# Gate and up products of two FFNs: plain block products against Strassen's form for two of four k-group pairs

## The chip, the core and the metric

The kernel runs on one core of one Trainium2 chip. The metric is the device time of one execution in microseconds; the kernel before takes 2469.53 us (median of three runs, 2468.38 to 2471.1). TensorE multiplies, VectorE (DVE) and ScalarE (ACT) work on elements, GpSimd (POOL) does little here, and the queue of SyncE (SP) issues all weight loads.

## The reference

Two transformer blocks run one after the other on x of 256 tokens by 2048 features, in fp32. The first has three mixers, then a gated FFN with a short convolution, then a gated per-layer input; the second has two mixers and a SwiGLU FFN, and a final norm. The change concerns the FFNs:

```python
def conv_ffn(x, w_gate, w_up, conv_w, conv_b, w_down):
    hg = x @ w_gate                      # [256, 2048] @ [2048, 5632]
    hg = conv_general_dilated(hg, conv_w, ..., feature_group_count=hg.shape[-1]) + conv_b
    return (gelu(hg) * (x @ w_up)) @ w_down

c = rmsnorm(h, ffn_norm); h = h + conv_ffn(c, w_gate, w_up, conv_w, conv_b, w_down)
...
h = rmsnorm_2(x, ffn_norm_w)
x = x + (silu(h @ w_gate) * (h @ w_up)) @ w_down
```

## The kernel before

Every product with a weight matrix is made in fp32 accuracy out of fp32r matmuls. An operand is split in two parts: hi is the value rounded to fp32r, lo is the rest. The product is hi x hi + hi x lo + lo x hi, three matmuls (lines 156 to 158), all added up in one PSUM bank.

The tokens are two tiles of 128 (m = 0, 1). The activations lie feature-major as 16 k-tiles xT of [128, 256], each already split. A weight is read in chunks of 512 columns and k groups of two k-tiles: a weight block is [128, 2 x 512] of fp32, 512 KB. `product` (line 160) walks the 8 k groups of a chunk. For each block SP loads it into one of seven buffers (three "raw", four "t4k"), ACT writes the rounded copy `whi` (line 133), VectorE writes `wlo = raw - whi` (line 134), and TensorE does 12 matmuls of 128x512: two k-tiles, two token tiles, three parts. There are three buffers each of `whi` and `wlo`.

An FFN has 11 chunks u of 512 hidden features. A unit makes gate chunk u and up chunk u, 8 blocks each (`conv_unit` line 556, `swiglu_unit` line 575); `evacuate` (line 236) takes a result out of PSUM scaled with the token's norm factor r. `hidden` then transposes it, applies convolution and GELU (or the SwiGLU product) and splits it into stationary tiles `hid`. Units go in groups (0,1), (2,3), ..., (10). After the two units of a group the down product of the group before is made: four output chunks of 8 blocks, each added to h by VectorE (line 541). Transposes and other small work are generators that `pump` advances at each weight block, so they fall between the blocks.

The order on each engine is set when the program is built: a scheduler places the instructions by priority (a split has high priority) and by its own estimate of when operands are ready. On the chip each engine runs its own list in that order, with semaphores for the waits. PSUM has eight banks: four "acc" for products, four "tp" for transposes and small products.

Of the kernel before, what the change touches and what calls it, by code (L numbers as in the profile page):

```python
# [17 lines left out]
P = 128  # L18
T = 256
# [34 lines left out]
def two_blocks_kernel(ctx: ExitStack, tc: tile.TileContext, A: dict, out: bass.AP):  # L54
# [105 lines left out]
    def product(w, c, xs, k0=0, order=None, width=2):  # L160
        """acc[m] = xs^T @ w[k-tiles k0.., chunk c] for both token tiles m."""
        n = w.widths[c]
        acc = [psum("acc"), psum("acc")]
        groups = order if order is not None else list(range(len(xs) // KG))
        for gi, g in enumerate(groups):
            while any(x is None for x in xs[g * KG : g * KG + KG]):
                pump()
            hi, lo = split_weight(w, c, k0 // KG + g)
            for j in range(KG):
                xhi, xlo = xs[g * KG + j]  # L170
                first = gi == 0 and j == 0
                last = gi == len(groups) - 1 and j == KG - 1
                wh, wl = hi[:, j * n : (j + 1) * n], lo[:, j * n : (j + 1) * n]
                for m in range(2):
                    three_products(acc[m][:, :n], xhi, xlo, m, wh, wl, first, last)
            pump(width)
        return acc

    def stationary(src, tag, scale=None):
        """Exact two-part split of a feature-major [128, 256] operand."""  # L180
        hi = new([P, T], tag, 32, F32R)
        lo = new([P, T], tag, 32, F32R)
        if scale is None:
            act(hi, src, AF.Copy)  # L184
            dve.tensor_tensor(lo, src, hi.bitcast(F32), op=ALU.subtract)
        else:
            act(hi, src, AF.Copy, scale=scale)
            dve.scalar_tensor_tensor(lo, src, scale, hi.bitcast(F32), ALU.mult, ALU.subtract)
        return hi, lo

    def transpose_pair(views, dst=None):
        """Two token-major [128, 128] views side by side, feature-major, in PSUM."""
        t = psum() if dst is None else dst
        for m, v in enumerate(views):
            pe.transpose(t[:, m * P : (m + 1) * P], v, ident)  # L195
        return t[:, :T]

    def norm_chunk(c, g, st):
        """Sums of squares of h[c], and its k-tiles, transposed and scaled by the gain."""
        for kk in range(4):  # L200
            if kk == 2:
                yield 1
            k = c * 4 + kk
            t = transpose_pair([h[c][:, m, kk * P : (kk + 1) * P] for m in range(2)])
            st.xs[k] = stationary(t, "xT", g[:, k : k + 1])
# [6 lines left out]
    class NormState:  # L212
        def __init__(self):
# [12 lines left out]
    def token_r(st):  # L226
# [99 lines left out]
    def hgrn_head(hh):  # L326
# [182 lines left out]

    # --- MOBA: one block of 256 keys, so the own block is the whole causal range  # L510
    def moba_bias(hh):
# [30 lines left out]

    def residual_norm(w, xin, g, order=None):
        """h += xin @ w, and the transposed scaled h for the next products."""
        st = NormState()
        for c in range(NCH):
# [3 lines left out]

    ahead[0] = True
    xs, r = residual_norm(W["out"], mix, G_FFN)

    # ================================================================== block 1: conv FFN
    def conv_unit(u, xs, r):
        gt = evacuate(product(W["gate"], u, xs), r)
        ut = evacuate(product(W["up"], u, xs), r)

# [15 lines left out]

    def swiglu_unit(u, xs, r):
        sg = evacuate(product(W["gate2"], u, xs), r, func=AF.Silu)
        acc = product(W["up2"], u, xs)
        for m in range(2):
            dve.scalar_tensor_tensor(sg[:, m], acc[m], r[:, m : m + 1], sg[:, m], ALU.mult, ALU.mult)

# [10 lines left out]

    def ffn(unit, down, xs, r, g):
        groups = [(0, 1), (2, 3), (4, 5), (6, 7), (8, 9), (10,)]
        prev = None
        st = NormState() if g is not None else None

        def drain(u0, hid, last):
            if last and g is None:
                return final_rows(down, u0, hid)
            for c in range(NCH):  # L600
# [11 lines left out]
        drain(*prev, True)  # L612
        return (st.xs, st.r) if g is not None else None
# [47 lines left out]
    w = W["in2"]  # L661
    # --- GLA
    gm = load_matrix("gla_m", 1152, "cm")
# [385 lines left out]
```

## Time and profile before

| | |
|---|---|
| median of three runs | 2469.53 us |
| span of the profiled execution | 2464.9 us |
| TensorE matmul busy | 2441.0 us, 11424 instructions |
| VectorE busy | 1421.2 us, 1767 instructions |
| ScalarE busy | 1219.1 us, 1705 instructions |
| granted TensorE clock, mean | 0.999 |
| read from memory | 444.76 MB, mean 181 GB/s |

The profile records one execution. Its own device time isn't listed beside it; its span runs from the first to the last instruction and is 4.6 us shorter than the median. Times are in microseconds from the start of the span, means of single instructions in ns. A matmul's recorded duration (about 0.39 us) is longer than the distance to the next one, since matmuls are pipelined; the distance is what counts for throughput.

### The profile page before, as it was taken

What the parts mean: (1) busy time and instruction counts of PE and PEld (TensorE: products, weight loads), DVE (VectorE), ACT (ScalarE), POOL (GpSimd) and SP (SyncE); (2) the same over time, 40 slices, a digit from 0 to 9 for tenths busy, and PEclk for the clock granted to TensorE, in tenths of its full rate; (3) what the DMA queues carried; (4) which work ended last, traced back from release to release, by engine and by line L of the source; (5) the groups of instructions that cost most, each with busy time, mean ns of one, the idle gap of its engine ahead of it and who ended that gap; (6) DMA issues with size and microseconds to landing.
All of it is one profiled execution on the core that took longest, in us unless ns stands there. A gap on an engine that the chain in (4) does not pass through costs nothing.

```text
span 2464.9 us, 30001 instructions
## 1 busy us (share of the span) xinstructions
PE 2441.0 (99%) x11424; PEld 2015.9 (82%) x11424; DVE 1421.2 (58%) x1767; ACT 1219.1 (49%) x1705; POOL 20.6 (1%) x26
## 2 busy tenths in 40 slices
PE   9999999999999999999999999999999999999998
PEld 7878888888888888888887888788888888888886
DVE  6786565555555465555656755655545545454556
ACT  6545454455445454544556555654444443434444
POOL 0000000000000000000000000000000000000000
PEclk9999999999999999999999999999999999999999
DMA  7544565555555656555545465555565555655554
GB/s 241 145 144 151 179 205 187 186 184 185 186 191 182 195 179 193 187 186 186 183 152 179 153 197 186 165 160 186 191 191 188 189 190 191 191 188 189 188 195 141
DMA packets 130654, 448.86 MB, mean 182 GB/s; under 512 B 14860, under 2 KB 19852, under 8 KB 130510
## 3 DMA queue, kind: packets, MB, share of 16 engines
q1 hardware_dynamic: 130510, 446.95, 57.1%
q8 instruction: 89, 1.46, 0.2%
q14 instruction: 55, 0.45, 0.1%
HBM read 444.76 MB, written 2.13 MB: 181 GB/s over the span
## 4 chain that ended last, share of the span: by engine, by line
PE 94%; DVE 2%; DMA 1%; issue 1%; ACT 1%; SPq 0%; POOL 0%; POOLq 0%; DVEq 0%; ACTq 0%
PE acc L158 30%; PE acc L156 30%; PE acc L157 29%; PE tp L195 2%; DVE wlo L134 1%; ACT whi L133 1%; DMA mbias<-vdr 1%; PE tp L358 0%; DMA raw<-in_w_down 0%; PE tp L860 0%; DVE t2k L835 0%; PE tp L845 0%; DMA raw<-in_w_in 0%; DMA h<-in_x 0%; DVE at L367 0%
## 5 line engine op out<-in xcount | busy, mean ns | idle before, releaser
L156 PE MATMUL acc<-whi,xT 128*128 128x512 f32 (+3 forms) x2400 | 935.8, 390 | 0.0
L158 PE MATMUL acc<-whi,xT 128*128 128x512 f32 (+3 forms) x2400 | 924.4, 385 | 0.0
L157 PE MATMUL acc<-wlo,xT 128*128 128x512 f32 (+3 forms) x2400 | 924.2, 385 | 0.0
L134 DVE TENSOR_TENSOR wlo<-raw,whi 128x1024 fp32r<-128x1024 f32 (+3 forms) x483 | 575.1, 1191 | 521.0 <-ACT whi L133 520.2
L133 ACT ACTIVATE whi<-raw 128x1024 fp32r<-128x1024 f32 (+3 forms) x483 | 498.8, 1033 | 590.0 <-PE acc L158 523.0
L134 DVE TENSOR_TENSOR wlo<-t4k,whi 128x1024 fp32r<-128x1024 f32 x353 | 432.7, 1226 | 439.6 <-ACT whi L133 439.3
L133 ACT ACTIVATE whi<-t4k 128x1024 fp32r<-128x1024 f32 x353 | 374.3, 1060 | 481.0 <-PE acc L158 461.1
L158 PEld LDWEIGHTS acc<-whi,xT 128*128 128x128 f32 x2400 | 451.1, 188 | 90.6 <-issue 0.9
L156 PEld LDWEIGHTS acc<-whi,xT 128*128 128x128 f32 x2400 | 451.3, 188 | 87.7 <-issue 2.9
L157 PEld LDWEIGHTS acc<-wlo,xT 128*128 128x128 f32 x2400 | 451.8, 188 | 86.3 <-DVE wlo L134 0.7
L156 PE MATMUL acc<-whi,hid 128*128 128x512 f32 x944 | 376.4, 399 | 0.0
L157 PE MATMUL acc<-wlo,hid 128*128 128x512 f32 x952 | 370.9, 390 | 0.0
L158 PE MATMUL acc<-whi,hid 128*128 128x512 f32 x944 | 370.3, 392 | 0.0
L158 PEld LDWEIGHTS acc<-whi,hid 128*128 128x128 f32 x944 | 177.2, 188 | 40.9
L157 PEld LDWEIGHTS acc<-wlo,hid 128*128 128x128 f32 x952 | 179.0, 188 | 37.6 <-DVE wlo L134 0.3
L156 PEld LDWEIGHTS acc<-whi,hid 128*128 128x128 f32 x944 | 177.5, 188 | 34.8 <-issue 0.4
L236 ACT ACTIVATE pj<-acc,r 128x512 f32<-128x512 f32 (+3 forms) x96 | 63.5, 662 | 41.2 <-PE acc L158 41.2
L541 DVE TENSOR_TENSOR h<-h,acc 128x512 f32<-128x512 f32 x104 | 67.2, 681 | 0.0
L195 PE MATMUL tp<-ident,pj 128*128 128x128 f32 x344 | 54.7, 273 | 1.2 <-DVE t2k L835 1.2
L195 PEld LDWEIGHTS tp<-ident,pj 128*128 128x128 f32 x344 | 43.4, 140 | 14.7 <-DVE t2k L835 1.6
L413 ACT ACTIVATE t2k<-t2k,col 128x256 f32<-128x256 f32 (+1 forms) x56 | 26.8, 480 | 23.7 <-DVE col L412 23.6
L184 ACT ACTIVATE hid<-t1k 128x256 fp32r<-128x256 f32 x44 | 18.3, 416 | 35.6 <-DVE t1k L570 35.6
(229 smaller groups left out, 1083.0 us busy)
## 6 DMA issues: line engine op xcount, KB each, us to landing
raw<-in_w_in SPq DMA_DIRECT2D x184, 512.0 KB, 3.6
t4k<-in_w_gate SPq DMA_DIRECT2D x100, 512.0 KB, 3.5
t4k<-in_w_up SPq DMA_DIRECT2D x100, 512.0 KB, 3.4
t4k<-in_w_down SPq DMA_DIRECT2D x96, 512.0 KB, 3.5
raw<-in_w_down SPq DMA_DIRECT2D x80, 512.0 KB, 3.4
raw<-in_w_gate SPq DMA_DIRECT2D x76, 512.0 KB, 3.5
raw<-in_w_up SPq DMA_DIRECT2D x76, 512.0 KB, 3.5
t4k<-in_w_out SPq DMA_DIRECT2D x37, 512.0 KB, 3.5
```

The source lines that it names most:

```text
L133: act(hi[:, :n], raw[:, :n], AF.Copy)
L134: dve.tensor_tensor(lo[:, :n], raw[:, :n], hi[:, :n].bitcast(F32), op=ALU.subtract)
L156: pe.matmul(o, xhi[:, tok], wh, start=first, stop=False)
L157: pe.matmul(o, xhi[:, tok], wl, start=False, stop=False)
L158: pe.matmul(o, xlo[:, tok], wh, start=False, stop=last)
L184: act(hi, src, AF.Copy)
L195: pe.transpose(t[:, m * P : (m + 1) * P], v, ident)
L236: act(t[:, m, :n], acc[m][:, :n], func, scale=r[:, m : m + 1])
L413: act(lg[:, a:b], lg[:, a:b], AF.Exp, bias=nm[:, m : m + 1], accum_out=sm[:, m : m + 1])
L541: dve.tensor_tensor(h[c][:, m], h[c][:, m], acc[m], op=ALU.add)
```

## The change

For units 2 to 10 of both FFNs gate and up of a chunk are made together in `pair_product`. The k groups are taken in pairs (gp, gp + 4), gp = 0..3. Pairs 0 and 2 stay plain ("straight"): four blocks of 12 matmuls into the banks p2, q4 (gate) and q3, x22 (up). Pairs 1 and 3 are "mixed". There the 2x2 block matrix of activations (rows: token tiles; columns: the two k groups) is multiplied with the 2x2 block matrix of weights b11, b12, b21, b22 (rows: the two k groups; columns: gate, up) by Strassen's seven products. VectorE forms sums of whole weight blocks in place: t1 = b11 + b12, t3 = b12 + b22, t2 = t1 + b22, t4 = t2 + b21. Seven blocks f11, f21, f22, ft1, ft3, ft2, ft4 are split and each is multiplied with one [128, 128] stationary pair per k-tile, 6 matmuls, into banks p1, p2, q3, q5, q7, q6, q4. All eight PSUM banks are in use during a unit. At its end nine operations of ACT and VectorE combine the banks into ca (gate) and cb (up), which ACT then scales by r in place.

The stationary combinations of activations are made once for each FFN by `strassen_operands` (four k-tile pairs, kept in four of the eight "pj" tiles) beside units 0 and 1, which stay plain. The down product of the group before is made in halves: two output chunks after each unit of a group, instead of four after the second. `norm_chunk` gets copies of h scaled by the norm factor of the norm before (rho) for the FFN norms, and the new r is divided by rho.

```diff
+    def split_raw(raw):
+        hi, lo = new([P, KG * 512], "whi", 3, F32R), new([P, KG * 512], "wlo", 3, F32R)
+        act(hi, raw, AF.Copy)
+        dve.tensor_tensor(lo, raw, hi.bitcast(F32), op=ALU.subtract)
+        return hi, lo
+    def pair_product(wa, wb, u, xs, sx):
+        p1, p2, q3, q5 = (psum("acc") for _ in range(4))
+        q6, q7, x22, q4 = (psum() for _ in range(4))
...
+        def products(bank, st, wt, stop):
+            (shi, slo), (hi, lo) = st, wt
+            for j in range(KG):
+                wh, wl = hi[:, j * 512 : (j + 1) * 512], lo[:, j * 512 : (j + 1) * 512]
+                pe.matmul(bank, shi(j), wh, start=id(bank) not in begun, stop=False)
+                begun.add(id(bank))
+                pe.matmul(bank, shi(j), wl, start=False, stop=False)
+                pe.matmul(bank, slo(j), wh, start=False, stop=stop and j == KG - 1)
...
+            last = gp == MIXED[-1]
+            b11, b12, b21, b22 = (load_weight(w_, u, g) for g in (gp, gp + half) for w_ in (wa, wb))
+            with tc.high_priority():
+                f11 = split_raw(b11)
+                t1 = b11
+                dve.tensor_tensor(t1, b11, b12, op=ALU.add)
+                f21 = split_raw(b21)
+                f22 = split_raw(b22)
+                t3 = b12
+                dve.tensor_tensor(t3, b12, b22, op=ALU.add)
+            products(p1, plain(gp, 0), f11, last)
+            products(p2, plain(gp + half, 0), f21, last)
+            products(q3, mixed(gp, 3), f22, last)
+            with tc.high_priority():
+                ft1 = split_raw(t1)
+                t2 = b22
+                dve.tensor_tensor(t2, t1, b22, op=ALU.add)
+                ft3 = split_raw(t3)
+                t4 = b21
+                dve.tensor_tensor(t4, t2, b21, op=ALU.add)
+            products(q5, mixed(gp, 0), ft1, last)
+            products(q7, mixed(gp, 2), ft3, last)
+            with tc.high_priority():
+                ft2 = split_raw(t2)
+            products(q6, mixed(gp, 1), ft2, last)
+            with tc.high_priority():
+                ft4 = split_raw(t4)
+            products(q4, plain(gp + half, 1), ft4, last)
+        ca, cb = chunk_tile(), chunk_tile()
+        with tc.high_priority():
+            a1, w_ = t2k(), t2k()
+            act(a1, p1, AF.Copy)
+            dve.tensor_tensor(ca[:, 0], a1, p2, op=add)
+            dve.tensor_tensor(a1, a1, q6, op=add)
+            dve.scalar_tensor_tensor(w_, a1, -1.0, q5, ALU.mult, add)
+            dve.tensor_tensor(cb[:, 0], w_, q3, op=add)
+            dve.tensor_tensor(a1, a1, q7, op=add)
+            dve.tensor_tensor(w_, w_, q7, op=sub)
+            dve.tensor_tensor(cb[:, 1], w_, x22, op=add)
+            dve.tensor_tensor(ca[:, 1], a1, q4, op=add)
...
         for us in groups:
             hid = [None] * (4 * len(us))
             for i, u in enumerate(us):
-                add_side(fill(hid, 4 * i, unit(u, xs, r)))
-            if prev is not None:
-                drain(*prev, False)
+                add_side(fill(hid, 4 * i, unit(u, xs, r, sx if u > 1 else None)))
+                if prev is not None:
+                    step = NCH // len(us)
+                    drain(*prev, range(i * step, (i + 1) * step))
```

How the order moves. On VectorE, where a unit's gate product follows a down product in the first FFN, the kernel before has one row a weight block (L134) and the two additions to h at the end of a down chunk (L541), nothing else:

```order
L134 TENSOR_TENSOR wlo_6833<-t4k_6830,whi_6832 128x1024
L134 TENSOR_TENSOR wlo_6851<-raw_6848,whi_6850 128x1024
L541 TENSOR_TENSOR h_5_70<-h_5_70,acc_6752 128x512
L541 TENSOR_TENSOR h_5_70<-h_5_70,acc_6753 128x512
L134 TENSOR_TENSOR wlo_6869<-raw_6866,whi_6868 128x1024
L134 TENSOR_TENSOR wlo_6887<-raw_6884,whi_6886 128x1024
L134 TENSOR_TENSOR wlo_6905<-t4k_6902,whi_6904 128x1024
```

In the kernel after, the first mixed pair of a unit reads as follows (L601 is the subtraction of a split; L645, L649, L656, L659 are t1, t3, t2, t4; the last row belongs to the next straight block):

```order
L601 TENSOR_TENSOR wlo_6034<-t4k_6025,whi_6033 128x1024
L645 TENSOR_TENSOR t4k_6025<-t4k_6025,t4k_6027 128x1024
L649 TENSOR_TENSOR t4k_6027<-t4k_6027,raw_6031 128x1024
L601 TENSOR_TENSOR wlo_6039<-t4k_6029,whi_6038 128x1024
L601 TENSOR_TENSOR wlo_6043<-raw_6031,whi_6042 128x1024
L656 TENSOR_TENSOR raw_6031<-t4k_6025,raw_6031 128x1024
L601 TENSOR_TENSOR wlo_6066<-t4k_6025,whi_6065 128x1024
L601 TENSOR_TENSOR wlo_6071<-t4k_6027,whi_6070 128x1024
L601 TENSOR_TENSOR wlo_6088<-raw_6031,whi_6087 128x1024
L659 TENSOR_TENSOR t4k_6029<-raw_6031,t4k_6029 128x1024
L601 TENSOR_TENSOR wlo_6098<-t4k_6029,whi_6097 128x1024
L134 TENSOR_TENSOR wlo_6110<-raw_6107,whi_6109 128x1024
```

Four of the eleven rows are sums; t1 and t3 stand before f21's subtraction, t2 before ft1's, t4 before ft4's. The second mixed pair of a unit, from t2 on, also holds combinations (L674 is ca, L675 a1 with q6, L676 w):

```order
L656 TENSOR_TENSOR raw_6185<-t4k_6179,raw_6185 128x1024
L674 TENSOR_TENSOR pj_6261<-t2k_6263,acc_5946 128x512
L601 TENSOR_TENSOR wlo_6220<-t4k_6179,whi_6219 128x1024
L601 TENSOR_TENSOR wlo_6225<-t4k_6181,whi_6224 128x1024
L601 TENSOR_TENSOR wlo_6242<-raw_6185,whi_6241 128x1024
L659 TENSOR_TENSOR raw_6183<-raw_6185,raw_6183 128x1024
L675 TENSOR_TENSOR t2k_6263<-t2k_6263,tp_5949 128x512
L676 SCALAR_TENSOR_TENSOR t2k_6264<-t2k_6263,acc_5948 128x512
L601 TENSOR_TENSOR wlo_6252<-raw_6183,whi_6251 128x1024
L134 TENSOR_TENSOR wlo_6283<-raw_6280,whi_6282 128x1024
```

The combination ca moved in ahead of ft1's subtraction, and a1 and w ahead of ft4's. On TensorE, before, a gate product begins right behind another product (acc_6978), its first block's matmuls in a row (acc_7126 and acc_7127 are the two token tiles):

```order
L157 MATMUL acc_6978<-wlo_7108,xT_4097 128x512
L158 MATMUL acc_6978<-whi_7107,xT_4098 128x512
L156 MATMUL acc_7126<-whi_7130,xT_3516 128x512
L157 MATMUL acc_7126<-wlo_7131,xT_3516 128x512
L158 MATMUL acc_7126<-whi_7130,xT_3517 128x512
L156 MATMUL acc_7127<-whi_7130,xT_3516 128x512
L157 MATMUL acc_7127<-wlo_7131,xT_3516 128x512
L158 MATMUL acc_7127<-whi_7130,xT_3517 128x512
```

After, at the end of a unit's second mixed pair (tp_5949 is q6's bank, tp_5952 q4's; tp_6316 takes over q6's bank; acc_6278 and acc_6279 are the down product's), the rows are:

```order
L619 MATMUL tp_5949<-whi_6241,pj_4228 128x512
L195 MATMUL tp_6316<-ident_63,pj_6261 128x128
L616 MATMUL tp_5952<-whi_6251,xT_4106 128x512
L156 MATMUL acc_6278<-whi_6282,hid_5192 128x512
L156 MATMUL acc_6279<-whi_6282,hid_5192 128x512
L618 MATMUL tp_5952<-wlo_6252,xT_4106 128x512
L619 MATMUL tp_5952<-whi_6251,xT_4107 128x512
L616 MATMUL tp_5952<-whi_6251,xT_4113 128x512
L618 MATMUL tp_5952<-wlo_6252,xT_4113 128x512
L619 MATMUL tp_5952<-whi_6251,xT_4114 128x512
L157 MATMUL acc_6278<-wlo_6283,hid_5192 128x512
```

A transpose of ca that writes into q6's former bank stands ahead of q4, and the first matmuls of the down product stand between q4's first and its other five, which need ft4's `wlo`.

## Rows read from the trace of the kernel before

**Rows 1.** The page's head: span, and busy time, share and instructions of each engine.
```profile
span 2464.9 us, 30001 instructions
PE 2441.0 (99%) x11424; PEld 2015.9 (82%) x11424; DVE 1421.2 (58%) x1767; ACT 1219.1 (49%) x1705; POOL 20.6 (1%) x26
```
**Rows 2.** Waits, whole span: engine, line, releaser: us in total, times, longest.
```profile
ACT whi L133 <- PE acc L158: 984.1, 612, 3.6
DVE wlo L134 <- ACT whi L133: 959.5, 733, 3.4
```
**Rows 3.** Timeline of TensorE, first FFN: start us, us, instruction (two stretches).
```profile
1001.26 0.40 PE L157 MATMUL acc<-wlo,xT 128*128 128x512 f32 x1
...
1003.57 0.40 PE L158 MATMUL acc<-whi,xT 128*128 128x512 f32 x1
...
1013.41 0.39 PE L158 MATMUL acc<-whi,xT 128*128 128x512 f32 x1
...
1020.89 0.39 PE L158 MATMUL acc<-whi,xT 128*128 128x512 f32 x1
```
**Rows 4.** Groups of VectorE and ACT by form: count, busy us, mean ns, idle before.
```profile
L134 DVE TENSOR_TENSOR wlo<-t4k,whi 128x1024 fp32r<-128x1024 f32 x353 | 432.7, 1226 | 439.6 <-ACT whi L133 439.3
L541 DVE TENSOR_TENSOR h<-h,acc 128x512 f32<-128x512 f32 x104 | 67.2, 681 | 0.0
L579 DVE SCALAR_TENSOR_TENSOR pj<-acc,r,pj 128x512 f32<-128x512 f32 x22 | 15.4, 743 | 0.0
L637 DVE TENSOR_TENSOR h<-h,pj 128x512 f32<-128x512 f32 x8 | 5.5, 687 | 0.0
L236 ACT ACTIVATE pj<-acc,r 128x512 f32<-128x512 f32 x88 | 59.8, 680 | 39.7 <-PE acc L158 39.7
```
**Rows 5.** Timeline of VectorE and ACT, w_out's and the first FFN's products.
```profile
382.89 1.28 DVE L541 TENSOR_TENSOR h<-h,acc 128x512 f32<-128x512 f32 x2
...
999.80 0.48 DVE L567 SCALAR_TENSOR_TENSOR t1k<-tp,cols,t1k 128x255 f32<-128x255 f32 x1
1000.32 0.48 DVE L568 SCALAR_TENSOR_TENSOR t1k<-tp,cols,t1k 128x254 f32<-128x254 f32 x1
...
1000.79 1.06 ACT L133 ACTIVATE whi<-t4k 128x1024 fp32r<-128x1024 f32 x1 [1.71 <-PE acc L158]
1001.75 0.40 ACT L569 ACTIVATE t1k<-t1k 128x256 f32<-128x256 f32 x1
...
1011.53 1.23 DVE L134 TENSOR_TENSOR wlo<-raw,whi 128x1024 fp32r<-128x1024 f32 x1 [0.35 <-ACT whi L133]
1012.67 0.41 DVE L570 TENSOR_TENSOR t1k<-t1k,tp 128x256 f32<-128x256 f32 x1
...
1021.32 1.06 ACT L133 ACTIVATE whi<-t4k 128x1024 fp32r<-128x1024 f32 x1 [1.61 <-PE acc L158]
...
1022.41 1.23 DVE L134 TENSOR_TENSOR wlo<-t4k,whi 128x1024 fp32r<-128x1024 f32 x1 [1.45 <-ACT whi L133]
```
**Rows 6.** Timeline at the kernel's start: VectorE, weight load, matmul.
```profile
7.30 1.22 DVE L134 TENSOR_TENSOR wlo<-raw,whi 128x1024 fp32r<-128x1024 f32 x1 [0.81 <-ACT whi L133]
...
8.58 0.29 PEld L157 LDWEIGHTS acc<-wlo,xT 128*128 128x128 f32 x1 [0.15 <-DVE wlo L134]
...
8.95 0.63 PE L157 MATMUL acc<-wlo,xT 128*128 128x512 f32 x1
```
**Rows 7.** Windows: engines' busy time, then granted clock, DMA share, GB/s.
```profile
115.00:130.00 15.00, 13.77 (x102) 12.85 (x101) 13.51 (x22) 9.28 (x19) 0.71 (x1) 1.00 0.56 169
999.90:1013.40 13.50, 13.50 (x66) 11.13 (x65) 10.73 (x19) 8.36 (x15) 0.00 (x0) 1.00 0.49 161
1560.00:1570.00 10.00, 8.67 (x50) 6.73 (x49) 8.60 (x25) 8.36 (x23) 0.00 (x0) 1.00 0.58 182
2455.00:2460.00 5.00, 1.40 (x7) 0.80 (x5) 2.60 (x7) 2.03 (x5) 0.56 (x1) 0.84 0.00 0
```
**Rows 8.** DMA issues: instructions, KB of each, median us to landing.
```profile
t4k<-in_w_gate SPq DMA_DIRECT2D x100, 512.0 KB, 3.5
```

More of the change, by code (lines that the diff above doesn't have):

```diff
@@ L198, in norm_chunk @@
     def norm_chunk(c, g, st):
+        rows = [h[c][:, m] for m in range(2)]
+        if st.rho is not None:
+            rows = [t2k(), t2k()]
+            for m in range(2):
+                act(rows[m], h[c][:, m], AF.Copy, scale=st.rho[:, m : m + 1])
         for kk in range(4):
@@ L203, in norm_chunk @@
             k = c * 4 + kk
-            t = transpose_pair([h[c][:, m, kk * P : (kk + 1) * P] for m in range(2)])
+            t = transpose_pair([rows[m][:, kk * P : (kk + 1) * P] for m in range(2)])
             st.xs[k] = stationary(t, "xT", g[:, k : k + 1])
@@ L231, in token_r @@
         pool.tensor_tensor(st.r, ms, mhalf[:, :2], op=ALU.pow)
+        if st.rho is not None:
+            inv = new([P, 2], "rinv", 2)
+            dve.reciprocal(inv, st.rho)
+            dve.tensor_tensor(st.r, st.r, inv, op=ALU.mult)
     def evacuate(acc, r, n=512, func=AF.Copy, dst=None):
@@ L541, in add_to_h, with residual_norm @@
             dve.tensor_tensor(h[c][:, m], h[c][:, m], acc[m], op=ALU.add)
[L543 to L545 removed]
+    def residual_norm(w, xin, g, rho, order=None):
+        st = NormState(rho)
         for c in range(NCH):
@@ L551, in two_blocks_kernel, with strassen_operands, make @@
     ahead[0] = True
[L552 to L557, printed above, removed]
+    xs, r = residual_norm(W["out"], mix, G_FFN, r)
+    def strassen_operands(xs):
+        sx = {}
+        def make():
+            for gp in MIXED:
+                for k in range(gp * KG, gp * KG + KG):
+                    while xs[k] is None or xs[k + 8] is None:
+                        yield 1
+                    yield 1
+                    a, b = t1k(), t1k()
+                    for t, (hi, lo) in ((a, xs[k]), (b, xs[k + 8])):
+                        dve.tensor_tensor(t, hi.bitcast(F32), lo.bitcast(F32), op=ALU.add)
+                    a11, a21, a12, a22 = a[:, :P], a[:, P:], b[:, :P], b[:, P:]
+                    fm = t2k()
+                    d, s2, s3, s4 = (fm[:, i * P : (i + 1) * P] for i in range(4))
+                    dve.tensor_tensor(d, a21, a22, op=ALU.subtract)
+                    dve.tensor_tensor(s2, d, a11, op=ALU.subtract)
+                    dve.tensor_tensor(s3, a11, a21, op=ALU.subtract)
+                    dve.tensor_tensor(s4, s2, a12, op=ALU.add)
+                    x = chunk_tile(F32R)
+                    act(x[:, 0], fm, AF.Copy)
+                    dve.tensor_tensor(x[:, 1], fm, x[:, 0].bitcast(F32), op=ALU.subtract)
+                    sx[k] = x
+        add_side(make(), 1)
+        return sx
@@ new lines, in two_blocks_kernel, with plain, mixed @@
+    MIXED = (1, 3)
+    def split_raw(raw):
[6 more added lines that the diff above has]
+        q6, q7, x22, q4 = (psum() for _ in range(4))
+        begun = set()
+        def products(bank, st, wt, stop):
[6 more added lines that the diff above has]
+                pe.matmul(bank, slo(j), wh, start=False, stop=stop and j == KG - 1)
+        def plain(g, m):
+            tok = slice(m * P, (m + 1) * P)
+            return lambda j: xs[g * KG + j][0][:, tok], lambda j: xs[g * KG + j][1][:, tok]
+        def mixed(gp, i):
+            fs = slice(i * P, (i + 1) * P)
+            return lambda j: sx[gp * KG + j][:, 0, fs], lambda j: sx[gp * KG + j][:, 1, fs]
+        half = KT // KG // 2
+        straight = [gp for gp in range(half) if gp not in MIXED]
+        for gp in range(half):
+            if gp in straight:
+                for w_, banks in ((wa, (p2, q4)), (wb, (q3, x22))):
+                    for g in (gp, gp + half):
+                        wt = split_weight(w_, u, g)
+                        for m in range(2):
+                            stop = banks[m] is x22 and g == straight[-1] + half
+                            products(banks[m], plain(g, m), wt, stop)
+                continue
+            last = gp == MIXED[-1]
[27 more added lines that the diff above has]
+        ca, cb = chunk_tile(), chunk_tile()
+        add, sub = ALU.add, ALU.subtract
+        with tc.high_priority():
[9 more added lines that the diff above has]
+            dve.tensor_tensor(ca[:, 1], a1, q4, op=add)
+        return ca, cb
@@ L559, in hidden, with conv_unit @@
+    def conv_unit(u, xs, r, sx):
+        if sx is None:
+            gt = evacuate(product(W["gate"], u, xs), r)
+            ut = evacuate(product(W["up"], u, xs), r)
+        else:
+            gt, ut = pair_product(W["gate"], W["up"], u, xs, sx)
+            for t in (gt, ut):
+                for m in range(2):
+                    act(t[:, m], t[:, m], AF.Copy, scale=r[:, m : m + 1])
         def hidden(kk):
@@ L573, in conv_unit, with swiglu_unit @@
         return hidden
-    def swiglu_unit(u, xs, r):
-        sg = evacuate(product(W["gate2"], u, xs), r, func=AF.Silu)
-        acc = product(W["up2"], u, xs)
+    def swiglu_unit(u, xs, r, sx):
+        if sx is None:
+            sg = evacuate(product(W["gate2"], u, xs), r, func=AF.Silu)
+            up = product(W["up2"], u, xs)
+        else:
+            sg, ut = pair_product(W["gate2"], W["up2"], u, xs, sx)
+            for m in range(2):
+                act(sg[:, m], sg[:, m], AF.Silu, scale=r[:, m : m + 1])
+            up = [ut[:, m] for m in range(2)]
         for m in range(2):
-            dve.scalar_tensor_tensor(sg[:, m], acc[m], r[:, m : m + 1], sg[:, m], ALU.mult, ALU.mult)
+            dve.scalar_tensor_tensor(sg[:, m], up[m], r[:, m : m + 1], sg[:, m], ALU.mult, ALU.mult)
         def hidden(kk):
@@ L595, in ffn, with drain @@
         st = NormState() if g is not None else None
[L597 to L600, printed above, removed]
+        sx = strassen_operands(xs)
+        def drain(u0, hid, chunks, last=False):
+            for c in chunks:
                 add_to_h(c, product(down, c, hid, k0=u0 * 4))
```

11 lines of the change are left out of this document (7 added, 4 removed).

## Prediction

> **What bounds the kernel now.** I read the page's head first, then the waits, then the timeline of TensorE in a unit of the first FFN. TensorE is busy for 2441.0 of 2464.9 us and VectorE for 1421.2 [rows 1]: the kernel is a stream of matmuls, and whatever shortens that stream counts in full as long as nothing else comes late. In the stretch with little beside the products 33 steps from one matmul to the next take 7.48 us, 0.227 each; where VectorE has other work too, ten take 2.31 us, 0.231 [rows 3]. I use p = 0.229 us for a 128x512 matmul. A weight block of 12 matmuls is then 2.75 us and four blocks 10.99 us.
>
> Next, what feeds TensorE. ACT rounds each weight block (whi), VectorE subtracts (wlo). ACT waits 984.1 us in all for matmuls, VectorE 959.5 us for ACT [rows 2]: the preparation is ready as early as the three buffers of whi and wlo allow and then sleeps, so it runs at most two blocks ahead. There is slack in total, but a lead of only some 5 us to spend at any one place.
>
> **What the change takes from TensorE.** A pair of k groups of gate and up is eight half blocks of 6 matmuls (48); Strassen's form needs seven (42). Two of the four pairs do so, in 9 units of each of two FFNs: 2 x 6 x 18 = 216 matmuls, which is also the difference of 128x512 rows in the two orders. 216 x 0.229 = 49.5 us, 2.75 per unit. This is the whole gain.
>
> **What it puts on VectorE.** A straight pair needs 4 subtractions. A mixed pair needs 7 subtractions and 4 sums of whole blocks, and the second mixed pair of a unit also holds three of the combinations (ca, a1, w). A subtraction of 128x1024 takes 1.226 us; a sum in place of two fp32 tiles is not there at that size, but at 128x512 it takes 0.687, against 0.681 to 0.743 with an operand in PSUM [rows 4]. Below, nothing makes the sum cheaper than the same elements of a subtraction; I take 1.23. Unwaited, the next operation starts 1.14 after a long one (1011.53 to 1012.67); one that needs the result starts 0.04 after its end (999.80 + 0.48 to 1000.32) [rows 5]. So a mixed pair is 11 x 1.14 = 12.5 us of VectorE or more, beside 42 x 0.229 = 9.6 us of TensorE. The straight pair before it leaves 10.99 - 4 x 1.14 = 6.4 us free, but only what the buffers allow can be done ahead.
>
> **The first mixed pair step by step.** Time 0 is the start of f11's products. Rules, all from rows: a buffer is free for ACT 0.20 after its block's last 0.229 step (a matmul lasts 0.39 and ACT starts 0.04 later: 1020.89 + 0.39 to 1021.32 [rows 3, 5]); ACT takes 1.06 and can start again after 0.96 [rows 5]; VectorE starts 0.03 after ACT's end; TensorE's matmul comes 0.25 after VectorE's or ACT's end. That last one is the weight load starting 0.06 after VectorE (7.30 + 1.22 to 8.58) plus about one warm step; the rows themselves show 0.43 to the matmul at the cold start and about 0.08 would be the least [rows 6].
> Ahead of time 0 VectorE does lo f11, t1, t3 and lo f21 (ending at 0.7), for f21 had to wait for the third straight block. f22's buffer comes free at 0.20: hi to 1.26, lo to 2.53, just in time for f22's products at 2.75. Then t2 (2.57 to 3.80), and only behind it lo ft1: 3.71 to 4.94, ready for TensorE at 5.19. f22's products ended at 4.12; TensorE fills two steps with the first matmuls of q5 and q7 (they need hi only), to 4.58, and waits 0.61. Lo ft3 ends at 6.08, lo ft2 at 7.22, both in time: q6 ends at 8.85. But t4 ends at 8.36, ACT rounds it 8.40 to 9.46, lo ft4 runs 9.50 to 10.73, ready at 10.98. TensorE does one matmul of q4 (9.71) and one of the next straight block, then the other five of q4 from 10.98 to 12.12. Less the borrowed step the pair took 11.89 us: 9.62 of matmuls and 2.27 of waits. The straight pair would have been 10.99. So +0.90.
>
> **The second mixed pair.** The same to t2. Then ca (0.68, 0.60 to the next) stands before lo ft1, which ends at 5.54; q5's rest goes 5.86 to 7.00 (the first matmul of q6 waited for hi ft2, 5.38 + 0.25). q7 and q6 follow without a wait, q6 ending at 9.29. Next on VectorE, ahead of lo ft4, is a1 += q6, which must see q6's last result: 9.49 to 10.17; then w on its result, 10.21 to 10.95; then lo ft4, 10.87 to 12.10, ready at 12.35. Ahead of q4 TensorE has a transpose that needs q6's bank, released only at 10.17. It does q4's first matmul, two of the down product (hi at 11.02 + 0.25), and q4's rest 12.35 to 13.50. Less the two borrowed steps and the transpose, 12.95 against 10.99: +1.96, of it 3.33 of waits.
>
> **The rest.** Third down block: the transposes of the new ca and cb stand inside it and wait for the scaling on ACT, some 0.3 us (ca's second half, then ACT 0.68 [rows 4]); bounds 0 and 1.5. Halving the down product moves whole blocks and adds no matmul. The four-block sums hold load buffers longer: the last is free at about 10.7 of a pair and its successor is wanted some 9 us later; loads land in 3.5 us [rows 8]: nothing, a few tenths if three queue up. Strassen's operands are about 2.7 us of VectorE for each of 8 k-tiles, beside the plain products of units 0 and 1 where VectorE is about half idle: nothing, at most 5 us in all. The scaled copies ahead of the norms are 32 ACT operations of at most 0.68; the k-tiles that they feed are due only six blocks into the next product: nothing, or 1 us.
> Sum per unit: 0.90 + 1.96 + 0.3 = +3.16; 18 units: +57 us. The page's execution spans 2464.9, 4.6 under the median of 2469.5 for what lies around the span. 2469.5 + 57 = 2526.5 us. With TensorE released 0.08 instead of 0.25 after its operand, some three exposed waits a unit shrink by 0.17: 9 us less. With 0.43, 10 more.
>
> **Two rules beside this.** VectorE's next operation starts 0.09 before the recorded end of the last [rows 5]. The Trainium skill ("VectorE: DVE Perf Modes", Terms) says a flush follows each operation and the next can't issue until the pipeline is empty; read as a step of the full 1.23, the chains t2 to lo ft4 would grow by about 0.7 us a unit, and the sum by 12 us. The rows show 1.14 here, so the sum keeps that. The other rule stands with the rivals.
>
> **Rivals.** (a) VectorE keeps up and the 49.5 us are gained: 2420. For it: over a whole unit VectorE has slack, since the down blocks need 1.14 in 2.75 us. Against: the order on VectorE and three buffers; in 115 to 130 us, with VectorE busy 13.51 of 15 us, TensorE loses 1.23 [rows 7]. It decides if the waits of a mixed pair stay near zero. 9%. (b) Break-even: waits of 1.37 us a mixed pair, as they would be if in the second pair the combinations slipped behind lo ft4: 2450 to 2490. 10%. (c) More waits, in the down blocks: VectorE is busy 10.73 of 13.5 us already while it makes the hidden tiles [rows 7], and five combinations of 0.68 fall into the same blocks. With 1.5 us lost in each half of the down product, 18 x 1.5 = 27 more: 2553. 15%. (d) TensorE's clock falls. It stayed at 1.00 where TensorE was busy only 8.67 of 10 us, and fell to 0.84 in the 5 us where TensorE was busy 1.40 [rows 7]; a mixed pair is busy about 0.78 of its time with gaps near 1 us, nearer the first. If each mixed pair ran at the lower level of 1.2 GHz, 36 pairs of 42 matmuls at twice 0.229 would be 19.2 us against some 12.4: 245 more, 2770. The Trainium skill ("TensorE: Matmul & The Clock Gate", the section on psum-queue depth-cycling) says that cycling PSUM banks with small idles between groups was enough to make the clock swing; by that rule this case would happen, and the rows of 1560 to 1570 speak against it. 4%. That the matmuls are not in fact fewer is excluded by the order.
>
> **How the numbers follow.** My forecast, waits on VectorE that cost twice what the matmuls save, has 62% and by itself 2505 to 2548. The range reaches into (b) and (c): 2478 to 2570; left out are (a), (d) and the tails. A measurement here can tell about 0.2%, 5 us. Slower than 2474: the forecast, (c), (d) and half of (b), 86%. Faster than 2465: (a) and a third of (b), 12%. The same: 2%.
>
> **What would show it.** Right: 216 fewer matmuls; in each mixed pair idle of TensorE put down to wlo and whi of the mixed splits (lines 600 and 601), little in the first half of a pair and 1 to 2 us ahead of q4's last five matmuls; VectorE nearly gapless through a mixed pair, its sums at 1.23; mixed pairs of about 11.9 and 13 us, straight ones 11; TensorE's clock at 1.00. Wrong: VectorE idle in the mixed pairs, sums well under 1.2, waits for DMA, or the loss sitting in the down blocks.

## The result, and the profile after

The changed kernel takes 2529.62 us (median of four runs, 2526.68 to 2533.07); the kernel before, beside it, 2468.95 us. The ratio is 1.0241, 95% interval 1.0229 to 1.0253: slower by 60.7 us, where 2526.5 us was forecast. One execution of a later run, the combinations without precedence, took 3022.74 us at a mean granted clock of 0.752 where its other three took 2504.74 to 2505.63 us; ratios leave it out. The head of the page and the shares of the chain that ended last:

```profile
span 2527.5 us, 30314 instructions
PE 2438.8 (96%) x11208; PEld 1969.5 (78%) x11208; DVE 1805.9 (71%) x2223; ACT 1347.4 (53%) x1855; POOL 20.8 (1%) x26
PE 84%; DVE 9%; ACT 3%; issue 2%; DMA 1%; SPq 0%; ACTq 0%; POOL 0%; POOLq 0%; DVEq 0%
```

The matmuls are fewer by the 216 that were worked out (11424 in [rows 1]), yet TensorE's busy time fell by only 2.2 us, not by 49.5. Most of the difference is in the records: a matmul in front of a wait or behind one is recorded as longer than its step (0.40 and 0.50 us at 636.03 and 637.05 below, for a step of 0.23). Some 5 us are matmuls at a lower clock (see *The clock* below). VectorE gained 384.7 us, and 9% of the chain now runs through it. The new waits (columns as in [rows 2]):

```profile
DVE wlo L134 <- ACT whi L133: 516.6, 440, 3.0
DVE wlo L601 <- ACT whi L600: 95.3, 90, 1.5
ACT whi L600 <- DVE t4k L659: 63.6, 21, 3.0
ACT whi L600 <- DVE raw L659: 45.7, 15, 3.3
PEld tp L616 <- ACT whi L600: 49.7, 44, 1.3
PEld acc L618 <- DVE wlo L601: 12.3, 18, 0.7
```

The first two lines answer to [rows 2]: of VectorE's 959.5 us of sleep behind ACT 612 are left. The rest is new. ACT waits up to 3.3 us for a sum (line 659 is t4), 36 times, once in each mixed pair. TensorE's weight loads wait for whi and wlo of the mixed splits, in the rows shown 44 and 18 times in 18 units.

One unit in windows: the first mixed pair, the straight pair, the second mixed pair, and two output chunks of the down product (four blocks each; the description of the kernel before says eight). The columns are from:to, length, busy time and count of TensorE, weight loads, VectorE, ACT and GpSimd, then granted clock, DMA share and GB/s.

```profile
627.51:639.35 11.84, 10.52 (x44) 7.73 (x42) 10.04 (x10) 7.21 (x7) 0.00 (x0) 1.00 0.41 128
639.35:650.24 10.89, 10.89 (x49) 9.01 (x48) 7.71 (x8) 4.25 (x4) 0.00 (x0) 1.00 0.74 248
650.24:663.00 12.76, 10.65 (x44) 7.67 (x43) 11.61 (x12) 8.18 (x9) 0.00 (x0) 1.00 0.35 121
663.55:687.02 23.47, 23.47 (x111) 18.99 (x111) 20.55 (x32) 14.99 (x23) 0.00 (x0) 1.00 0.65 223
```

Six matmuls fewer than the straight pair, and each mixed pair is longer than it: by 0.95 and by 1.87 us. The down product runs without a gap. The clock is at its higher level in these four windows; elsewhere in the span it fell three times (see *The clock* below).

In the first mixed pair the chain that ended last leaves TensorE altogether (start, us, what):

```profile
627.71 1.07 ACT whi L600
...
631.29 3.41 DVE wlo L601 x3
634.70 1.14 DVE t4k L659
...
637.03 0.92 DVE wlo L601
638.00 0.49 PE acc L616
```

From ACT's rounding of f22 on it is VectorE's queue, one operation behind the other, until ft4 is rounded and subtracted. VectorE and ACT in the same stretch (f11's products begin at 627.51; a number in brackets is idle time before, and what ended it):

```profile
628.80 1.23 DVE L601 TENSOR_TENSOR wlo<-t4k,whi 128x1024 fp32r<-128x1024 f32 x1 [0.56 <-ACT whi L600]
630.06 1.22 DVE L656 TENSOR_TENSOR t4k<-raw,t4k 128x1024 f32<-128x1024 f32 x1
631.21 2.35 DVE L601 TENSOR_TENSOR wlo<-raw,whi 128x1024 fp32r<-128x1024 f32 x2
633.48 1.22 DVE L601 TENSOR_TENSOR wlo<-t4k,whi 128x1024 fp32r<-128x1024 f32 x1
634.61 1.22 DVE L659 TENSOR_TENSOR t4k<-t4k,t4k 128x1024 f32<-128x1024 f32 x1
635.94 1.06 ACT L600 ACTIVATE whi<-t4k 128x1024 fp32r<-128x1024 f32 x1 [3.03 <-DVE t4k L659]
637.03 1.23 DVE L601 TENSOR_TENSOR wlo<-t4k,whi 128x1024 fp32r<-128x1024 f32 x1 [1.21 <-ACT whi L600]
```

t2 (line 656) stands ahead of ft1's subtraction (the first of the two at 631.21), t4 (line 659) behind three subtractions. What TensorE makes of it:

```profile
631.83 0.40 PE L616 MATMUL tp<-whi,pj 128*128 128x512 f32 x1
632.48 0.50 PE L618 MATMUL acc<-wlo,pj 128*128 128x512 f32 x1 [0.25 <-DVE wlo L601]
632.82 0.40 PE L619 MATMUL acc<-whi,pj 128*128 128x512 f32 x1
...
636.03 0.40 PE L619 MATMUL tp<-whi,pj 128*128 128x512 f32 x1
637.05 0.50 PE L616 MATMUL tp<-whi,xT 128*128 128x512 f32 x1 [0.62 <-ACT whi L600]
638.00 0.49 PE L616 MATMUL acc<-whi,xT 128*128 128x512 f32 x1 [0.44 <-ACT whi L133]
638.33 0.48 PE L618 MATMUL tp<-wlo,xT 128*128 128x512 f32 x1
```

The three holes are ft1's wlo (632.48), ft4's whi (637.05) and, behind one matmul borrowed from the next straight block (638.00), ft4's wlo (638.33). In the second mixed pair (from 650.24) VectorE has three combinations as well (lines 674 to 676):

```profile
653.94 0.68 DVE L674 TENSOR_TENSOR pj<-t2k,acc 128x512 f32<-128x512 f32 x1
654.53 1.22 DVE L601 TENSOR_TENSOR wlo<-raw,whi 128x1024 fp32r<-128x1024 f32 x1
...
657.94 1.22 DVE L659 TENSOR_TENSOR t4k<-t4k,t4k 128x1024 f32<-128x1024 f32 x1
659.69 0.69 DVE L675 TENSOR_TENSOR t2k<-t2k,tp 128x512 f32<-128x512 f32 x1 [0.53 <-PE tp L619]
660.41 0.69 DVE L676 SCALAR_TENSOR_TENSOR t2k<-t2k,acc 128x512 f32<-128x512 f32 x1
661.01 1.22 DVE L601 TENSOR_TENSOR wlo<-t4k,whi 128x1024 fp32r<-128x1024 f32 x1
```

The combination of line 674 delays ft1's subtraction by 0.59 us, and lines 675 and 676 stand ahead of ft4's. VectorE even sleeps 0.53 us there, since a1 += q6 has to see q6's last matmul.

### The profile page after: what moved, and what is told of

It is laid out like the page before. It is cut to its first block, busy times and chain, and to the rows that moved or that the text cites. A ratio compares the mean times of both kernels' runs of the same rounds, so it can differ in the third digit from the quotient of the medians.

```text
span 2527.5 us, 30314 instructions
## 1 busy us (share of the span) xinstructions
PE 2438.8 (96%) x11208; PEld 1969.5 (78%) x11208; DVE 1805.9 (71%) x2223; ACT 1347.4 (53%) x1855; POOL 20.8 (1%) x26
## 4 chain that ended last, share of the span: by engine, by line
PE 84%; DVE 9%; ACT 3%; issue 2%; DMA 1%; SPq 0%; ACTq 0%; POOL 0%; POOLq 0%; DVEq 0%
PE acc L158 18%; PE acc L157 18%; PE acc L156 18%; DVE wlo L601 5%; PE tp L618 4%; PE tp L619 4%; PE acc L616 4%; PE acc L618 4%; PE acc L619 4%; PE tp L616 4%; PE tp L195 2%; ACT whi L600 2%; DVE wlo L134 1%; DMA mbias<-vdr 1%; DVE t4k L659 0%
## 5 line engine op out<-in xcount | busy, mean ns | idle before, releaser
L134 DVE TENSOR_TENSOR wlo<-raw,whi 128x1024 fp32r<-128x1024 f32 (+3 forms) x421 | 497.8, 1184 | 337.0 <-ACT whi L133 331.8
L133 ACT ACTIVATE whi<-raw 128x1024 fp32r<-128x1024 f32 (+3 forms) x421 | 431.5, 1027 | 439.5 <-PE acc L158 323.2
L156 PE MATMUL acc<-whi,xT 128*128 128x512 f32 (+3 forms) x1248 | 483.6, 388 | 0.0
L157 PE MATMUL acc<-wlo,xT 128*128 128x512 f32 (+3 forms) x1248 | 475.5, 381 | 0.2 <-DVE wlo L134 0.2
L158 PE MATMUL acc<-whi,xT 128*128 128x512 f32 (+3 forms) x1248 | 475.0, 381 | 0.0
L134 DVE TENSOR_TENSOR wlo<-t4k,whi 128x1024 fp32r<-128x1024 f32 x271 | 330.2, 1223 | 185.7 <-ACT whi L133 184.7
L158 PEld LDWEIGHTS acc<-whi,xT 128*128 128x128 f32 x1248 | 234.9, 188 | 45.1 <-issue 0.9
L156 PEld LDWEIGHTS acc<-whi,xT 128*128 128x128 f32 x1248 | 235.0, 188 | 43.7 <-issue 2.9
L157 PEld LDWEIGHTS acc<-wlo,xT 128*128 128x128 f32 x1248 | 235.4, 189 | 42.4 <-DVE wlo L134 1.0
L601 DVE TENSOR_TENSOR wlo<-t4k,whi 128x1024 fp32r<-128x1024 f32 x143 | 172.6, 1221 | 54.1 <-ACT whi L600 54.1
L600 ACT ACTIVATE whi<-raw 128x1024 fp32r<-128x1024 f32 x109 | 115.1, 1060 | 133.3 <-PE tp L619 77.7
L616 PE MATMUL acc<-whi,xT 128*128 128x512 f32 x432 | 170.1, 394 | 8.0 <-ACT whi L133 8.0
L618 PE MATMUL acc<-wlo,xT 128*128 128x512 f32 x432 | 168.2, 389 | 0.0
L619 PE MATMUL acc<-whi,xT 128*128 128x512 f32 x432 | 168.1, 389 | 0.0
```

The costliest lines, as they stand in the source:

```text
L133: act(hi[:, :n], raw[:, :n], AF.Copy)
L134: dve.tensor_tensor(lo[:, :n], raw[:, :n], hi[:, :n].bitcast(F32), op=ALU.subtract)
L156: pe.matmul(o, xhi[:, tok], wh, start=first, stop=False)
L157: pe.matmul(o, xhi[:, tok], wl, start=False, stop=False)
L158: pe.matmul(o, xlo[:, tok], wh, start=False, stop=last)
L600: act(hi, raw, AF.Copy)
```

## Experiments

My theory: the loss is VectorE's four sums on the way of the splits, where three buffers allow no lead. The rivals: the other edits (halved down product, scaled copies, more banks) cost something; the form itself does (eight banks, operands, matmuls); VectorE's total work is the bound.

**Everything but Strassen's form.** All four pairs are straight, in the banks p2, q3, x22 and q4, and no operands are made; `pair_product`, the halved down product and the scaled copies stay.

```diff
-    MIXED = (1, 3)
+    MIXED = ()
...
-            dve.tensor_tensor(ca[:, 0], a1, p2, op=add)
+            act(ca[:, 0], p2, AF.Copy)
```

> All four pairs of k groups plain (no Strassen, no block sums, no operands for it); the joint gate and up product, its copies out of PSUM, the down product in halves and the scaled copies ahead of the norms stay as in the changed kernel. Theory (the loss sits in the mixed pairs, where VectorE feeds seven splits and four sums through three buffers): 2472 us, between 2466 and 2478, since the other edits cost nothing that shows. Rival (part of the 61 us comes from halving the down product, from taking gate and up together or from the norm copies): 2485 or more.

Measured 2471.14 us, ratio 1.0002 (0.9993 to 1.0011). The other edits cost nothing that shows; the 60.7 us belong to the mixed pairs, with their operands and their four more banks.

**The form without the sums.** The four sums of weight blocks are left out (ft1 to ft4 are the loaded blocks, so the product is another one); the rest of the program stays. The order on VectorE changed with it: in the trace a1 += q6 and w now stand behind ft4's subtraction.

```diff
-                dve.tensor_tensor(t1, b11, b12, op=ALU.add)
-                dve.tensor_tensor(t3, b12, b22, op=ALU.add)
-                dve.tensor_tensor(t2, t1, b22, op=ALU.add)
-                dve.tensor_tensor(t4, t2, b21, op=ALU.add)
```

> The four sums of weight blocks are left out (the splits take b11, b12, b22, b21 instead of t1, t3, t2, t4), so the numbers are not the product; all seven splits, 216 fewer matmuls and all combinations stay. Theory: without the sums VectorE needs 7 x 1.14 = 8.0 us for 9.6 us of matmuls, waits in the mixed pairs nearly vanish and the 49.5 us are gained: 2425 us, 2418 to 2440. Rival 1 (the splits themselves and the three buffers are enough to stall TensorE): above 2469. Rival 2 (the waits come from PSUM banks and the combinations at the end of a unit, not from the sums): about 2500.

Measured 2435.71 us, ratio 0.9858 (0.9844 to 0.9873). The first mixed pair now runs through, and one wait is left:

```profile
624.50:634.10 9.60, 9.60 (x43) 7.91 (x43) 7.38 (x7) 7.45 (x7) 0.00 (x0) 1.00 0.43 135
PEld acc L618 <- DVE wlo L601: 10.4, 18, 0.6
```

(The first line is from its windows, the second from its waits.) So 2529.62 - 2435.71 = 93.9 us hang on 144 sums, which occupy VectorE for 144 x 1.22 = 176 us, and on the order that they bring with them. The first mixed pair holds no combination and shows the sums alone: 9.60 us for 11.84, 2.24 a unit, 40 us in all. The other 54 us hold the sums of the second pair, the two combinations that moved, and the falls of the clock; these were not separated here. The remaining wait of 0.6 us, 18 times, is again for ft1's subtraction, in the second mixed pair, where the combination ca stands ahead of it. The gain is 34.4 us, not the 45 that I expected here: that wait explains 10 of the 15 us that are missing of 49.5; the other 5 stayed open.

**One mixed pair a unit.** Only the first, or only the second; the other is straight (in the first case the stop flags of some matmuls move with it).

```diff
-    MIXED = (1, 3)
+    MIXED = (1,)
```

> Only pair 1 of each unit is mixed, pairs 0, 2 and 3 are plain; the combinations then fall beside plain blocks. Theory: the first mixed pair alone loses 0.9 us against a plain one, 18 units: 2469 + 17 = 2486 us, 2480 to 2492. Rival (the two mixed pairs are alike, half of the loss each): 2499. Rival (a single mixed pair, with much lead on either side, gains its 1.37 us): 2444.

Measured 2487.36 us, ratio 1.0071 (1.0054 to 1.0087).

```diff
-    MIXED = (1, 3)
+    MIXED = (3,)
```

> Only pair 3 of each unit is mixed, pairs 0 to 2 are plain. Theory (each mixed pair loses on its own, the first by its sums, the second by sums and combinations): what the first pair does not explain of the loss, 60.7 - 17.2 = 43.5 us over the kernel before: 2512 us, 2505 to 2519. Rival (the second pair is slow because the first has used up the lead, and one plain pair does not restore it): 2485, like the first alone.

Measured 2507.15 us, ratio 1.0155 (1.0138 to 1.0172). Against the runs beside them that is +17.2 and +37.8 us, 0.96 and 2.10 a unit, for +0.90 and +1.96 (and 0.3 in the down block) in the prediction. Together they make 55.0 of the 60.7 us. In the usual units of the first FFN the two nearly add up: from one unit to the next it is 67.42 us before, 68.32 with the first pair mixed, 69.40 with the second, 70.40 with both. So little of the missing 5.7 us comes from the pairs acting on each other. Most of it is matched by the falls of the clock, some 5 us in the changed kernel's profile (see *The clock* below); neither of these two profiles has one.

**Combinations without precedence.** They are no longer put ahead of the splits.

```diff
-        with tc.high_priority():
-            a1, w_ = t2k(), t2k()
+        a1, w_ = t2k(), t2k()
```

> The combinations at the end of a unit lose their high priority and nothing else changes; in the order on VectorE ca moves behind t4 and w behind ft4's subtraction, while a1 += q6 stays ahead of it. Theory: in the second mixed pair ft4's subtraction ends at 10.9 instead of 12.1 us after the pair's start, 1.2 us less a unit, 18 units: 22 us less than the changed kernel, 2507 us, 2500 to 2517. Rival (what holds the second pair is q6's bank and the transpose ahead of q4, or the end of the unit as a whole): 2525 to 2535, no change. A loss above 2535 would mean that the combinations are then late for the transposes in the down blocks.

Measured 2505.26 us, ratio 1.0140 (1.0123 to 1.0156): 24.4 us less than the change, 1.35 a unit. Some 5 us of that may be falls of the clock, which would leave about 1.1 a unit. The combinations among the splits are thus about what the second pair costs more than the first (0.92 a unit in the windows, 1.14 between the two runs above).

**The sums ahead of the pair.** t1 and t2 go into two free "pj" tiles, so that b11 and b22 needn't be split before they are overwritten, and three sums are made before f11 is split. In the order a1 += q6 and w again stand behind ft4's subtraction.

```diff
+                t1 = chunk_tile().rearrange("p m n -> p (m n)")
+                dve.tensor_tensor(t1, b11, b12, op=ALU.add)
...
+                t2 = chunk_tile().rearrange("p m n -> p (m n)")
+                dve.tensor_tensor(t2, t1, b22, op=ALU.add)
+                f11 = split_raw(b11)
```

> All work of the changed kernel is kept. t1 and t2 are written into two free 4 KB tiles instead of over b11 and b22, so that t1, t3 and t2 need no split to come first; in the order on VectorE they stand among the plain blocks ahead of the mixed pair, and a1 += q6 stands behind ft4's subtraction. Theory (VectorE has the time, only not at that place): the waits go as they went without the sums, 2436 us, 2430 to 2455, faster than both kernels. Rival (VectorE is simply too full with 8 more sums a unit, wherever they stand, or the early sums wait for loads and hold the splits behind them): 2480 or more.

Measured 2436.61 us, ratio 0.9868 (0.9852 to 0.9884). VectorE is as busy as in the changed kernel (1805.9 us in both), and the kernel is 93 us faster than that: the place of the sums, and of the combinations that moved with them, decides, not their number. The form with its eight banks and VectorE's total work are the same as in the changed kernel, so neither costs this time by itself.

**The sums on GpSimd.** The same four lines on the engine that has little else to do.

```diff
-                dve.tensor_tensor(t2, t1, b22, op=ALU.add)
+                pool.tensor_tensor(t2, t1, b22, op=ALU.add)
```

> The four block sums are done by GpSimd instead of VectorE, nothing else is changed. No row so far shows how long GpSimd takes for a sum of 128x1024. Theory (the loss is VectorE's time): if a sum takes GpSimd under about 2.2 us, t1, t2 and t4 in a row are ready in time and the result is that of the kernel without sums, 2436 us, to 2450; if it takes 3 us or more, ft4 waits for t4 and the time lies above 2500. Rival (VectorE and GpSimd hinder each other): VectorE's subtractions would last longer than 1.23 us beside it.

Measured 2612.85 us, ratio 1.0582 (1.0566 to 1.0598), the slowest of the medians. Groups by form (busy, mean ns, idle before), then VectorE and GpSimd in one mixed pair:

```profile
L601 DVE TENSOR_TENSOR wlo<-t4k,whi 128x1024 fp32r<-128x1024 f32 x143 | 306.2, 2158 | 74.4 <-ACT whi L600 73.6
L645 POOL TENSOR_TENSOR raw<-raw,raw 128x1024 f32<-128x1024 f32 x10 | 24.0, 2400 | 328.0 <-DVE wlo L601 328.0
L659 POOL TENSOR_TENSOR t4k<-t4k,t4k 128x1024 f32<-128x1024 f32 x16 | 51.9, 3244 | 1.3
...
638.30 4.58 DVE L601 TENSOR_TENSOR wlo<-raw,whi 128x1024 fp32r<-128x1024 f32 x2
642.92 4.55 DVE L601 TENSOR_TENSOR wlo<-t4k,whi 128x1024 fp32r<-128x1024 f32 x2
...
638.51 3.28 POOL L656 TENSOR_TENSOR t4k<-raw,t4k 128x1024 f32<-128x1024 f32 x1 [1.21 <-DVE wlo L601]
641.87 3.25 POOL L659 TENSOR_TENSOR t4k<-t4k,t4k 128x1024 f32<-128x1024 f32 x1
```

Two subtractions that take 2.35 us alone take 4.58 with a sum of GpSimd beside them. The 2.2 us more are nearly what the quickest sum takes (2.40), and the sum is stretched in turn. So the two engines hardly worked at the same time, and VectorE was relieved of nothing: it is busy for 1874.1 us with 144 operations fewer, against 1805.9. The Trainium skill ("SBUF — State Buffer", on the two separate sides) says that VectorE and GpSimd share a pair of ports under an exclusive lock held for an instruction; the 4.58 us agree with that.

**A fourth buffer of whi and wlo.** Paid for by smaller scratch pools. The same was done to the kernel before, as its control.

```diff
-new([P, KG * 512], "whi", 3, F32R), new([P, KG * 512], "wlo", 3, F32R)
+new([P, KG * 512], "whi", 4, F32R), new([P, KG * 512], "wlo", 4, F32R)
...
-        return new([P, 512], "t2k", 8)
+        return new([P, 512], "t2k", 5)
...
-        return new([P, T], "t1k", 6)
+        return new([P, T], "t1k", 4)
```

> The changed kernel with four instead of three buffers of whi and wlo; for the space t2k has 5 instead of 8 buffers and t1k 4 instead of 6. Theory (the lead that the buffers allow is what runs out in a mixed pair): one block more of lead is 2.75 us, above the 2.3 us that the first mixed pair waits, and the order moves a1 and w behind ft4's subtraction: 2438 us, 2428 to 2460 with what the smaller scratch costs in the mixers. Rival (VectorE's total is what counts, the buffers do not matter): 2515 to 2530.

> The kernel before with four instead of three buffers of whi and wlo and the smaller scratch, no Strassen. Theory (a longer lead is worth something only where VectorE falls behind, and in plain products it never does): 2469 us, 2465 to 2474. Rival (the buffers speed up the kernel by themselves, so the 2421 us with four buffers are not the matmuls saved): 2440 or less.

The changed kernel with four buffers: 2421.36 us, ratio to before 0.9807 (0.9792 to 0.9822). The kernel before with four: 2467.95 us, 0.9994 (0.9985 to 1.0003). So the buffers by themselves do nothing, and with them the change is worth 47.6 us, about the 49.5 of its 216 matmuls: it beats both kernels. Its page and the first mixed pair:

```profile
span 2419.6 us, 30321 instructions
PE 2393.3 (99%) x11208; PEld 1974.2 (82%) x11208; DVE 1803.7 (75%) x2223; ACT 1352.4 (56%) x1855; POOL 20.8 (1%) x26
...
621.21:630.78 9.57, 9.57 (x43) 7.89 (x42) 9.33 (x9) 7.22 (x7) 0.00 (x0) 1.00 0.51 155
```

and VectorE in the pair, whose f11 products begin at 621.21:

```profile
621.42 1.22 DVE L656 TENSOR_TENSOR t4k<-raw,t4k 128x1024 f32<-128x1024 f32 x1
622.57 2.57 DVE L601 TENSOR_TENSOR wlo<-raw,whi 128x1024 fp32r<-128x1024 f32 x2
625.05 1.22 DVE L659 TENSOR_TENSOR t4k<-t4k,t4k 128x1024 f32<-128x1024 f32 x1
626.19 1.22 DVE L601 TENSOR_TENSOR wlo<-t4k,whi 128x1024 fp32r<-128x1024 f32 x1
```

VectorE has the same operations and nearly the same time in all (1803.7 us, against 1805.9), is as good as full in the pair (9.33 of 9.57 us), and TensorE doesn't wait. t2 starts 0.2 us into the pair instead of 2.5, t4 at 3.8 instead of 7.1: one more block could be split ahead. The gain went beyond my expectation. The new buffer count also moved the order: t4 now precedes one of the subtractions that it stood behind, and in the second pair, as expected, a1 and w stand behind ft4's subtraction. How much is the lead and how much the order was not separated.

## Why the prediction was right, and what it mis-sized

*Matmuls saved.* 216, as counted. With the waits gone (four buffers) they bring 47.6 us, for the 49.5 of the prediction.

*First mixed pair.* Against the start of f11's products, forecast and measured: lo f22 1.30, 1.29; t2 2.57, 2.55; lo ft1 3.71, 3.70; t4 7.13, 7.10; hi ft4 8.40, 8.43; lo ft4 9.50, 9.52; q4's second matmul 10.98, 10.82. The pair took 11.84 us for 11.89. The straight pair beside it is 10.89, not 10.99, so that the difference is +0.95 for +0.90. The run with this pair alone grows by 0.90 a unit (67.42 to 68.32).

*Second mixed pair.* Line 674 at 3.70 as t2's end demands; a1 += q6 9.45 for 9.49; w 10.17 for 10.21; lo ft4 10.77 for 10.87; the pair 12.76 for 12.95, so +1.87 for +1.96. The run with this pair alone grows by 1.98 a unit (67.42 to 69.40).

*The step of unwaited VectorE operations.* 1.13 and 1.14 us (633.48 to 634.61) beside durations of 1.22. The literal reading of the Trainium skill's flush rule ("VectorE: DVE Perf Modes", Terms), which would have added 12 us, is not borne out.

*Sums.* 1.22 to 1.23 us, as taken from subtractions: a sum in place of two fp32 blocks is no cheaper.

*The mis-sized term:* "TensorE's matmul comes 0.25 after VectorE's or ACT's end". It is 0.05, below even the 0.08 that the prediction gave as the least: ACT ends at 637.00, the matmul begins at 637.05; line 601's first of two ends near 632.44, the matmul begins at 632.48. The step after such a matmul is 0.34 (632.48 to 632.82) instead of 0.23, so that about 0.1 of the 0.2 comes back. The second pair, with most such waits, came out 0.19 shorter than forecast.

*Down blocks and the other edits.* In the down blocks the transposes wait at most 0.4 us for the scaling (0.3 forecast), in 9 of 18 units, 3.4 us in all: less than the 0.3 a unit of the sum. In the window from 663.55 TensorE is busy for 23.47 of 23.47 us: rival (c) is not seen at its own place. The other edits cost nothing that shows, as the run without mixed pairs has it (the scaled copies are 16, not 32).

*The clock.* It is 1.00 in the windows above, though TensorE is busy for only 10.65 of 12.76 us there and all eight banks go round. But three times it fell, each time while TensorE did the last products of a second mixed pair, right behind the waits ahead of them (windows as above; the two matmuls are from the second):

```profile
1155.00:1160.00 5.00, 4.78 (x14) 3.68 (x14) 4.33 (x5) 2.00 (x3) 0.00 (x0) 0.66 0.65 226
2100.00:2105.00 5.00, 4.81 (x14) 3.46 (x14) 4.43 (x5) 1.77 (x2) 0.00 (x0) 0.66 0.69 206
2380.00:2385.00 5.00, 4.82 (x14) 3.83 (x15) 4.82 (x6) 1.18 (x2) 0.00 (x0) 0.66 0.83 278
...
2101.09 0.63 PE L619 MATMUL tp<-whi,xT 128*128 128x512 f32 x1
2101.51 0.63 PE L616 MATMUL tp<-whi,xT 128*128 128x512 f32 x1
```

The step is 0.42 to 0.43 us there instead of 0.23, as at the lower level of 1.2 GHz, and some eight matmuls at 0.2 us more make about 1.6 us each time, some 5 us in all. So rival (d), which put all 36 mixed pairs at the lower level for 245 us, came true at 3 of them. The 15 other second pairs have waits of the same kind and kept the clock; what makes the difference no run shows. The times of the changed kernel's four executions go with the clock: 2526.68 us at a mean clock of 0.998, 2533.07 at 0.995. Nor does it take a mixed pair: the run without them has one such fall near 1358 us, in the second block's mixers, behind a wait of 1.82 us. The rule of the Trainium skill named with rival (d) ("TensorE: Matmul & The Clock Gate", psum-queue depth-cycling) would fit these three; at the 33 other mixed pairs the banks go round and the clock stays at 1.00.

*The sum.* Two units before take 134.85 us in the windows of one group, 67.4 each; after, from a unit's t2 to that of the next it is 70.4: +3.0 for +3.16 (66.5 and 69.4 in the second FFN). 18 x 3.0 is 54 of the 62.6 us by which the span grew. The rest, some 9 us, was not in the sum. About 5 are the falls of the clock: from the last addition to h of one group of two units to that of the next, the kernel grew by 5.7 to 6.2 us, but by 7.4 and 7.6 where the clock fell (its third fall is in a group of one unit). Some 3 lie in the first group with mixed pairs of each FFN, which grew by 7.7 and 7.3, and some 2 outside the FFNs; the cause of these is not settled. That the forecast came within some 3 us of the median is in part luck: these additions stand against the smaller unit. (The 4.6 us "for what lies around the span" are misread: each execution of the two kernels is some 1.9 us longer than its own span. The forecast starts from the median, so nothing in it hangs on that.)

*Rivals (a) and (b).* VectorE kept up only once it had a lead. Rival (a) put the question as one of total slack ("over a whole unit VectorE has slack"), and so it was for four buffers: the slack was there and out of reach with three.

## What to carry to other kernels

An operation that is cheap in total can put much of its time on the critical path if it stands in the queue of the engine that feeds the bound, within a burst whose lead the buffers limit (here 2.24 us of the 4.9 us of sums in a first mixed pair): set the feeder's time inside the burst (12.5 us) against the bound's (9.6 us) and ask how far ahead it may start. Before such a change is given up, or its work is moved to another engine, try one more buffer or an earlier place, and give the kernel before the same buffer as a control.

## What the runs showed of the hardware

In the mixed splits a matmul begins 0.05 us after the last writer of its operand has ended, and the step behind it is 0.33 to 0.35 instead of 0.23 us. Unwaited subtractions of 128x1024 fp32 on VectorE start 1.13 to 1.14 us apart, though each is recorded as 1.22. A GpSimd sum of 128x1024 fp32 took 2.40 us in the quickest of the four groups and 3.25 where VectorE ran beside it all the time; VectorE's subtractions went from 1.22 to a mean of 2.16 us. TensorE's granted clock fell to its lower level behind waits of under 1 us, in 3 of 18 stretches that look alike, with steps of 0.42 to 0.43 us instead of 0.23.
